# A two-layer fp32 encoder trunk on one core: 48 matmuls of the output projection move between the last units of the latent attention, and the ring of split weight tiles has nine places instead of eight

## The chip, the cores and the metric

One Trainium2 chip, one of its cores. The metric is device time in microseconds of one execution of the whole program, median of several runs.

## The reference

The input is 1024 tokens of width 1024 in fp32. There are two residual layers, each with a mixer and a squared-ReLU MLP of width 4096, and a final norm. The change touches the mixer of the second ("odd") layer: a latent attention of 8 heads beside a recurrent block, whose outputs, 512 wide each, are joined and go through one output projection.

```python
def dense_mla(qn, qr, kn, kr, v):
    ...
        s = (jnp.einsum('bqhd,bkhd->bhqk', qn_b, kn) + jnp.einsum('bqhr,bkr->bhqk', qr_b, kr)).astype(F32) * scale
        p = jax.nn.softmax(s, axis=-1).astype(v.dtype)
        return jnp.einsum('bhqk,bkhd->bqhd', p, v)

def odd_mixer(h, ...):
    ...
    yc = dense_mla(qn, qr, kn, rope(kr), v)
    yd = rglru_block(xr, xg, conv_w, conv_b, wa, ba, wx, bx, lam)
    return jnp.concatenate([yc, yd], axis=-1) @ w_out

def sq_relu_mlp(h, w1, w2):
    u = jax.nn.relu(h @ w1)
    return (u * u) @ w2
...
x = x + mixer(rmsnorm(x, norm_mix))
x = x + sq_relu_mlp(rmsnorm(x, norm_mlp[layer]), w_mlp1[layer], w_mlp2[layer])
```

## The kernel before

Activations lie transposed: 128 channels to a tile, 1024 tokens (S) along it, in two halves of N2 = 512 (`H2`). Results are wanted to fp32, and TensorE is fed in the type fp32r, so every operand is split in two: `split` (L132) writes hi, a cast of x to fp32r (L122, mostly on ScalarE), and lo = x - hi (L130, on VectorE or GpSimd, the latter called POOL in the profile). `mm3` (L179) then makes each product of three matmuls: hi·hi, hi·lo and lo·hi. In the trace a tile whose name ends in h or l is such a half.

The program is five phases: even mixer, MLP 0, odd mixer, MLP 1, final norm. It is written in a framework that tracks tiles: a named pool has a fixed number of places, and a tile that is to be written waits until the place that it gets is free of its former readers. A scheduler orders the instructions within each engine before the program runs, so the order on an engine isn't quite that of the code; on the chip each engine then goes through its own queue strictly in order, and an instruction that waits holds all behind it.

**The ring "w"** has W_BUFS = 8 places of 128 x 1024 fp32r. Through it go: the split weights wh and wl of `fetch` (L168), the weight blocks wb of the MLPs (`block`, L272), and in the attention the head values VS (`head_values`, L1315) and the transposed probabilities cpT (`mla_transpose`). `fetch` also takes one of RAW_BUFS = 2 places for the raw weight, which SP's queue loads by DMA. The list of weights to load (`requests`, from L137) is worked off in order, and `weight` (L164) always has two more ahead of the one it hands out. So o_w_out of m = 0 and m = 1 are split at the beginning of the attention and keep four places through all of it, and in each MLP the last weights of w2 do the same.

**The latent attention** has 32 steps (head h of 8, pair of query blocks p of 4), each of four units kk, so units u = 0 to 127. Each unit issues the pieces of ODD_STEP = ("P", "S", "T", "V"):

- P: a piece of the next head's preparation, up to head 7.
- S: every second unit, the scores of two steps further on (`mla_scores`: six matmuls into the two-bank tile ms, a maximum on VectorE, the exponential e with the sum csm on ScalarE), and in the units between, the normalising of e on POOL (`norm`).
- T: four transposes of e into the PSUM tile ctp, a cast to cpT's first half on ScalarE (L1353) and the difference to its second half on VectorE (L1354).
- V: `av` of the unit four earlier (ODD_LAG = 4): eight matmuls from VS and cpT into the PSUM tile cav (L1124); at the end of every second step a copy cavl on ScalarE (L1131) and a sum into yc.

After the loop stand, in the code, the splits of yd (the recurrent block's output, tiles th to yh and yl, k = 4 to 7; cast on ScalarE, subtraction on POOL), the loads of X (the residual, eight DMAs on SP's queue), `av` of the last four units, the splits of yc (k = 0 to 3), and the projection:

```python
order = [4, 5, 6, 7, 0, 1, 2, 3]
for n in range(2):
    for m0 in range(0, NC, 2):
        W = [self.weight(), self.weight()]
```

For each token half n and each pair of output blocks m it opens two PSUM tiles op, does part 0 (the four k of yd) and part 1 (the four k of yc), 24 matmuls for each m, and adds to X. `done` then squares X for the next norm. The weights are asked for twice over, m = 0 to 7 for n = 0 and again for n = 1.

**The MLPs** are block products with sums and differences of blocks (a scheme of fewer products). Their weights come through `w_stream`, are split to wb (cast on ScalarE L122, difference on VectorE L130) in the ring "w", and are used in twelve matmuls each: in L378 for the first half (PSUM tiles q, copied out to t in L396, among others) and in L498 for the second half (inputs ub).

Of the kernel before, what the change touches and what calls it, by code (L numbers as in the profile page):

```python
# [15 lines left out]
P = 128  # L16
# [30 lines left out]
class Trunk:  # L47
# [89 lines left out]
    def requests(self, ph):  # L137
# [6 lines left out]
        if ph == "odd":  # L144
            idx = {"xr3": 6, "ckv": 2, "cq0": 0, "cq1": 1, "xg0": 7, "xg1": 8, "xg2": 9, "xg3": 10}
            late = {"kn": (a["w_uk"], N2), "qr": (a["w_uq_r"], N2), "qn": (a["w_uq_n"], S), "vn": (a["w_uv"], N2)}
            r = [(a["o_w_in"][i], S, "act" if i != 5 else "pool") for i in (3, 4, 5)]
            seen = set()
            for op in ODD_START:
                k = op[:-1]  # L150
                if k in seen:
                    continue
                seen.add(k)
                if k in idx:
                    r.append((a["o_w_in"][idx[k]], S, "pool"))
                elif k in late:
                    r.append(late[k])
            return r + [(a["o_w_out"][m], S, "act", "pool") for m in range(NC)] * 2
        if ph == "final":
# [8 lines left out]
    def fetch(self, ahead):  # L168

        while self.wreq and len(self.wout) < ahead:  # L170
            src, n, *eng = self.wreq.pop(0)
            raw = self.wp.tile([P, S], F32, tag="raw", name=self.nm("raw"), bufs=RAW_BUFS)
            self.nc.sync.dma_start(raw[:, :n], src)
            h = self.wp.tile([P, S], F32R, tag="w", name=self.nm("wh"))
            l = self.wp.tile([P, S], F32R, tag="w", name=self.nm("wl"))
            self.split(h[:, :n], l[:, :n], raw[:, :n], *eng)
            self.wout.append((h, l))
# [94 lines left out]
    def block(self, tag, x, le="dve", neg=False):  # L272

        nc = self.nc
        w = self.wp.tile([P, S], F32R, tag="w", name=self.nm(tag)) if tag == "wb" else self.G(tag, F32R)
        h, l = w[:, :N2], w[:, N2:]
# [640 lines left out]
    def odd(self, nb, xs, nxt):  # L917
# [195 lines left out]
        def av(u):  # L1113
# [13 lines left out]
            if p % 2 == 1 and kk == 3:  # L1127
                if h % 2 == 0 and p == 1:
# [5 lines left out]
                                        tmp[0:64], op=ALU.add)  # L1134

        prep = iter(())
        for u in range(4 * NS):
            i, kk = divmod(u, 4)
            h, p = steps[i]
            for op in ODD_STEP:  # L1140
# [11 lines left out]
                elif op == "V":  # L1152
                    av(u - ODD_LAG)
                elif op == "P":
                    if p == 0 and kk == 0 and 1 <= h < 7:
                        prep = prep_qk(h + 1)
                    next(prep, None)
            if p == 1 and kk == 3 and h < 7:
                VS[h + 1] = self.head_values(h + 1, Vn)
        Yh, Yl = [None] * 8, [None] * 8  # L1160
        for c in range(4):
            Yh[4 + c], Yl[4 + c] = self.G("yh", F32R), self.G("yl", F32R)
            for s in H2:
                self.split(Yh[4 + c][:, s], Yl[4 + c][:, s], yd[c][:, s], "act", "pool")
        X = self.load_x(xs)
        for u in range(4 * NS - ODD_LAG, 4 * NS):
            av(u)
        for k in range(4):
            Yh[k], Yl[k] = self.G("yh", F32R), self.G("yl", F32R)
# [5 lines left out]
        for n in range(2):  # L1175
            for m0 in range(0, NC, 2):
                W = [self.weight(), self.weight()]
                grp = [(m0 + j, self.PS("op")) for j in range(2)]
                for part in range(2):
                    ks = order[4 * part:4 * part + 4]  # L1180
# [134 lines left out]
    def head_values(self, h, Vn):  # L1315
        nc = self.nc
        VS = self.wp.tile([P, S], F32R, tag="w", name=self.nm("VS"))
        vv = VS.rearrange("p (b t d) -> p b t d", b=8, t=2)
# [25 lines left out]
    def mla_transpose(self, pr, kk):  # L1344
        nc = self.nc
        tp = self.PB("ctp")
        for i in range(2):
            for j in range(2):
                kb = 2 * kk + i
                nc.tensor.transpose(tp[:, (2 * i + j) * P:(2 * i + j + 1) * P], pr[j][:, kb * P:(kb + 1) * P],  # L1350
                                    self.ident)
        pp = self.wp.tile([P, S], F32R, tag="w", name=self.nm("cpT"))
        nc.scalar.copy(pp[:, :N2], tp)  # L1353
# [328 lines left out]
G_BUFS = 41  # L1682
W_BUFS = 8
RAW_BUFS = 2
# [127 lines left out]
```

## Time and profile before

| | |
|---|---|
| median of 3 runs | 2158.83 us (2158.75 to 2159.36) |
| profiled execution, its own time | 2161.66 us |
| its span, first to last instruction | 2159.5 us |
| mean granted TensorE clock | 0.987 |
| TensorE busy | 2051.3 us, 95% of the span |
| VectorE, ScalarE, POOL busy | 71%, 49%, 38% |

The span is what the trace shows; the profiled execution's own time is 2.2 us longer, and 2.8 us longer than the median of the runs without a profile. PE in the profile is TensorE's matmuls and PEld its weight loads, which overlap them; DVE is VectorE, ACT ScalarE, SP the engine whose queue issues the loads. A row of groups gives line, engine, operation, output<-inputs with the count, then shortest, median and longest duration in ns (or busy us and mean ns). In the trace the attention's regular part ends near 1402 us, the projection near 1494 us.

### The profile page before, as it was taken

The page shows a single profiled execution, that of the slowest core. Times are in us where ns is not written, and L with a number is a line of the kernel's source. Part 1 is how long each engine was busy: PE and PEld are TensorE (multiplying, and loading weights), DVE is VectorE, ACT ScalarE, POOL GpSimd, SP SyncE. Part 2 cuts the span into 40 slices and gives each one's busy share as a digit, 9 for nine tenths or more (in the row PEclk, how much of TensorE's full clock was granted, in tenths as well). Part 3 has the DMA queues.
Part 4 walks back from the last instruction along what each step waited for, and adds up shares of the span by engine and source line. Part 5 has one row for each costly group of instructions (what it writes and reads, how often), then busy time and mean ns, then how long its engine had stood idle before and what let it go on. Part 6 is the DMA issues. An engine that isn't in the chain of part 4 may idle for free.

```text
span 2159.5 us, 27248 instructions
## 1 busy us (share of the span) xinstructions
PE 2051.3 (95%) x9600; PEld 1688.1 (78%) x9600; DVE 1542.9 (71%) x2365; ACT 1065.0 (49%) x1853; POOL 823.2 (38%) x635
## 2 busy tenths in 40 slices
PE   6989998999999999999997999999899999999997
PEld 5867776787777888888785898888678777788887
DVE  7688868765656877775898888717875655877964
ACT  5236645444544534340565777734645545544423
POOL 4133332332315142242557776463242321522414
PEclk9999999999999999999999999999999999999999
DMA  5630052543448535132102000245443445654302
GB/s 176 144 136 24 11 185 78 176 166 127 151 152 310 176 107 180 55 101 76 35 25 68 11 11 10 79 130 188 135 172 127 152 155 179 236 204 157 127 29 79
DMA packets 115544, 261.32 MB, mean 121 GB/s; under 512 B 19664, under 2 KB 21840, under 8 KB 115408
## 3 DMA queue, kind: packets, MB, share of 16 engines
q1 hardware_dynamic: 115408, 259.59, 35.7%
q8 instruction: 75, 1.23, 0.2%
q14 instruction: 61, 0.50, 0.1%
HBM read 178.28 MB, written 72.35 MB: 116 GB/s over the span
## 4 chain that ended last, share of the span: by engine, by line
PE 72%; DVE 12%; issue 5%; ACT 5%; DMA 3%; POOL 3%; SPq 0%; POOLq 0%; DVEq 0%; ACTq 0%
PE q L498 22%; PE q L378 22%; PE op L185 7%; PE z L185 6%; PE ms L1334 4%; PE o L185 3%; PE cav L1124 2%; PE ctp L1350 2%; DVE th L1443 1%; POOL acc L245 1%; DVE wb L130 1%; DMA X<-xm 1%; DMA raw<-in_e_w_in_dram 1%; PE tp L870 1%; DVE w L1433 0%
## 5 line engine op out<-in xcount | busy, mean ns | idle before, releaser
L378 PE MATMUL q<-hb,wb 128*128 128x512 f32 x2688 | 629.7, 394 | 34.6 <-DVE wb L130 9.8
L378 PEld LDWEIGHTS q<-hb,wb 128*128 128x128 f32 x2688 | 504.1, 189 | 158.2 <-DVE wb L130 12.8
L498 PE MATMUL q<-ub,wb 128*128 128x512 f32 x2352 | 539.3, 391 | 8.8 <-ACT wb L122 7.0
L498 PEld LDWEIGHTS q<-ub,wb 128*128 128x128 f32 x2352 | 443.2, 189 | 104.3 <-ACT wb L122 8.8
L130 DVE TENSOR_TENSOR wb<-raw,wb 128x512 fp32r<-128x512 f32 x268 | 226.6, 851 | 112.6 <-ACT wb L122 112.2
L122 ACT CAST wb<-raw 128x512 fp32r<-128x512 f32 x268 | 164.3, 619 | 183.0 <-PE q L378 112.7
L122 ACT CAST wb<-sum 128x512 fp32r<-128x512 f32 x152 | 93.8, 620 | 183.3 <-PE q L378 100.7
L130 DVE TENSOR_TENSOR ub<-ut,ub 128x512 fp32r<-128x512 f32 x168 | 136.3, 824 | 66.2 <-ACT ub L122 65.8
L122 ACT CAST ub<-ut 128x512 fp32r<-128x512 f32 x168 | 101.4, 618 | 147.2 <-DVE wb L130 18.8
L130 DVE TENSOR_TENSOR wb<-sum,wb 128x512 fp32r<-128x512 f32 x152 | 126.3, 833 | 22.5 <-ACT wb L122 21.5
L185 PE MATMUL z<-Hh,wh 128*128 128x512 f32 x328 | 129.8, 400 | 10.6 <-ACT wh L122 9.6
L245 POOL TENSOR_TENSOR acc<-acc,sq 128x512 f32<-128x512 f32 (+1 forms) x62 | 88.3, 1427 | 123.3 <-ACT sq L244 121.4
L185 PE MATMUL z<-Hl,wh 128*128 128x512 f32 x328 | 130.2, 397 | 4.1 <-DVE Hl L1471 4.0
L185 PE MATMUL z<-Hh,wl 128*128 128x512 f32 x328 | 129.1, 394 | 0.8 <-DVE wl L130 0.8
L323 POOL TENSOR_TENSOR sum<-raw,raw 128x512 f32<-128x512 f32 x28 | 40.3, 1448 | 215.6 <-DMA raw<-in_w_dram 184.4
L332 POOL TENSOR_TENSOR raw<-raw,raw 128x512 f32<-128x512 f32 x32 | 43.5, 1360 | 203.2 <-DVE wb L130 175.6
L1124 PE MATMUL cav<-cpT,VS 128*128 128x256 f32 x512 | 102.7, 305 | 3.6 <-ACT cpT L1353 2.3
L122 ACT CAST wh<-raw 128x1024 fp32r<-128x1024 f32 (+1 forms) x49 | 49.8, 1015 | 111.9 <-PE z L185 39.4
L1334 PE MATMUL ms<-Kt,Qt 128*128 128x512 f32 (+1 forms) x384 | 99.8, 396 | 2.2 <-ACT e L1341 1.4
L185 PE MATMUL op<-yh,wh 128*128 128x512 f32 x252 | 100.0, 398 | 1.4 <-DVE ya L887 0.9
L185 PE MATMUL op<-yl,wh 128*128 128x512 f32 x252 | 98.9, 393 | 0.0
L185 PE MATMUL op<-yh,wl 128*128 128x512 f32 x252 | 98.0, 393 | 0.0
(343 smaller groups left out, 3815.0 us busy)
## 6 DMA issues: line engine op xcount, KB each, us to landing
raw<-in_w_dram SPq DMA_DIRECT2D x140, 512.0 KB, 4.5
xm<-X SPq DMA_DIRECT2D x32, 256.0 KB, 2.0
X<-xm SPq DMA_DIRECT2D x16, 512.0 KB, 6.6
raw<-in_o_w_out_dram SPq DMA_DIRECT2D x16, 512.0 KB, 3.5
raw<-in_o_w_in_dram SPq DMA_DIRECT2D x11, 512.0 KB, 3.5
raw<-in_e_w_in_dram SPq DMA_DIRECT2D x10, 512.0 KB, 5.1
X<-in_x_dram SPq DMA_DIRECT2D x16, 256.0 KB, 5.6
raw<-in_e_w_out_dram SPq DMA_DIRECT2D x8, 512.0 KB, 3.6
```

Source lines behind the costliest of these rows:

```text
L122: self.nc.scalar.copy(out, x)
L130: e.tensor_tensor(out, x, y, op=ALU.subtract)
L185: self.nc.tensor.matmul(ps, l, r, start=(first and i == 0), stop=(last and i == n - 1))
L245: (eng or nc.gpsimd).tensor_tensor(acc, acc, sq, op=ALU.add)
L323: add(x, blk(p, 1, 0), blk(p, 1, 1), op=ALU.add)
L332: add(x, x, blk(p, 1, 0), op=ALU.add)
L378: nc.tensor.matmul(ps, a, b, start=(first and c == 0 and i == 0), stop=(c == 3 and i == 2), skip_group_check=True)
L498: nc.tensor.matmul(ps[m], a, b, start=(first and j == 0 and i == 0), stop=(j == len(pairs) - 1 and i == 2), skip_group_check=True)
L870: nc.tensor.transpose(tp[:, h * P:(h + 1) * P], pt[h // 2][:, o:o + P], self.ident)
L1124: nc.tensor.matmul(ACC[0][:, (p % 2) * 256:(p % 2 + 1) * 256], VS[h][:, kb * P:(kb + 1) * P], pp[:, t * N2 + ii * 256:t * N2 + (ii + 1) * ...
L1334: nc.tensor.matmul(ps[:, s], l[rows, qs], r[rows, s], start=(i == 0), stop=(i == 2))
L1350: nc.tensor.transpose(tp[:, (2 * i + j) * P:(2 * i + j + 1) * P], pr[j][:, kb * P:(kb + 1) * P], self.ident)
```

## The change

Four things are changed.

1. The splits of yd (k = 4 to 7, in halves) are issued from the loop, in the even units 96 to 110, instead of after it.
2. In the units 105, 109, 113 and 117 `out_weights` loads for m = 0 to 3 the second half of o_w_out[m], which is the four k of yd, as 128 x 512, and splits it into a tile ow (hi in the first half of the tile, lo in the second) of the general pool, which has 41 places, not of the ring. `requests` in turn asks only for the first halves of these four weights (N2 wide) for n = 0, and as before for all else.
3. From unit 120 on, P calls the generator `out_early`, which opens two PSUM tiles of two banks each, and does part 0 of n = 0 for m = 0 to 3: 48 matmuls, six to a call; what is left follows behind the last `av`. The projection takes these four tiles over and does only part 1 in them.
4. W_BUFS is 9.

```diff
+            return r + [(a["o_w_out"][m][:, :N2], N2, "act", "pool") for m in range(4)] + \
+                [(a["o_w_out"][m], S, "act", "pool") for m in [*range(4, NC), *range(NC)]]
...
+        def y_split(c, s):
+            if s.start == 0:
+                Yh[4 + c], Yl[4 + c] = self.G("yh", F32R), self.G("yl", F32R)
+            self.split(Yh[4 + c][:, s], Yl[4 + c][:, s], yd[c][:, s], "act", "pool")
+
+        def out_weights(m):
+            raw = self.H2("owr", "owr")
+            dma(raw, a["o_w_out"][m][:, N2:])
+            w = self.G("ow", F32R)
+            self.split(w[:, :N2], w[:, N2:], raw, "act", "pool")
+            early[m] = [w]
+
+        def out_early():
+            two = [self.PS2("op"), self.PS2("op")]
+            for m in range(4):
+                w = early[m][0]
+                ps = two[m // 2][:, (m % 2) * N2:(m % 2 + 1) * N2]
+                early[m].append(ps)
+                for k in range(4):
+                    cs, lo = slice(k * P, (k + 1) * P), slice(N2 + k * P, N2 + (k + 1) * P)
+                    self.mm3(ps, [(w[:, cs], w[:, lo], Yh[4 + k][:, H2[0]], Yl[4 + k][:, H2[0]])], k == 0, False)
+                    if k % 2:
+                        yield
...
+                    if 96 <= u < 112 and u % 2 == 0:
+                        y_split((u - 96) // 4, H2[u // 2 % 2])
+                    if 104 <= u < 120 and u % 4 == 1:
+                        out_weights((u - 104) // 4)
+                    if u >= 120:
+                        next(fill, None)
...
+                ready = n == 0 and m0 < 4
+                grp = [(m0 + j, early[m0 + j][1] if ready else self.PS("op")) for j in range(2)]
+                for part in range(1 if ready else 0, 2):
...
-W_BUFS = 8
+W_BUFS = 9
```

The scheduler takes these up in its own order. Three places of it follow. A row is line, operation, output<-inputs, size, and a count where rows repeat; numbers behind names count tiles, and lines of the changed kernel from 160 on are one to 34 higher.

ScalarE's queue near the splits of head 7's values (VS), in the attention's last third. Before:

```order
L1321 CAST VS_11843<-Vn_9483 128x2x64
L1321 CAST VS_11843<-Vn_9505 128x2x64
L1353 CAST cpT_11871<-ctp_11866 128x512
L1353 CAST cpT_11885<-ctp_11880 128x512
L1131 COPY cavl_11933<-cav_11781 64x512
L1341 ACTIVATE e_11948,csm_11945<-ms_11936,cnb_11944 128x1024
L1341 ACTIVATE e_11989,csm_11986<-ms_11977,cnb_11985 128x1024
```

And now:

```order
L1355 CAST VS_11855<-Vn_9483 128x2x64
L1355 CAST VS_11855<-Vn_9505 128x2x64
L1375 ACTIVATE e_11880,csm_11877<-ms_11868,cnb_11876 128x1024
L122 CAST ow_11896<-owr_11894 128x512
L1387 CAST cpT_11887<-ctp_11882 128x512
L1387 CAST cpT_11906<-ctp_11901 128x512
L1375 ACTIVATE e_11927,csm_11924<-ms_11915,cnb_11923 128x1024
L1132 COPY cavl_11956<-cav_11791 64x512
L1387 CAST cpT_11934<-ctp_11929 128x512
L122 CAST yh_11959<-th_9062 128x512 x2
L1387 CAST cpT_11948<-ctp_11943 128x512
```

The two exponentials that stood in a row behind the copy cavl now stand apart, with two casts of cpT between them, and the casts of ow and yh stand among those of cpT.

TensorE's queue in the last units of the attention, where no scores are left. Before, with the beginning of the projection at the end of the piece:

```order
L1124 MATMUL cav_12240<-cpT_12237,VS_11843 128x256 x3
L1124 MATMUL cav_12240<-cpT_12250,VS_11843 128x256
L1350 MATMUL ctp_12269<-ident,e_12112 128x128
L1350 MATMUL ctp_12269<-ident,e_12153 128x128
L1350 MATMUL ctp_12269<-ident,e_12112 128x128
L1350 MATMUL ctp_12269<-ident,e_12153 128x128
L1124 MATMUL cav_12240<-cpT_12250,VS_11843 128x256 x3
L1124 MATMUL cav_12240<-cpT_12262,VS_11843 128x256 x4
L185 MATMUL op_12377<-yh_12281,wh_9376 128x512
L185 MATMUL op_12377<-yl_12282,wh_9376 128x512
```

And now, some units earlier:

```order
L186 MATMUL op_12224<-yh_11667,ow_12078 128x512
L186 MATMUL op_12224<-yh_11764,ow_12078 128x512
L186 MATMUL op_12224<-yl_11765,ow_12078 128x512
L186 MATMUL op_12224<-yh_11764,ow_12078 128x512
L186 MATMUL op_12224<-yh_11864,ow_12078 128x512
L1384 MATMUL ctp_12197<-ident,e_11975 128x128
L1384 MATMUL ctp_12197<-ident,e_12022 128x128
L1384 MATMUL ctp_12197<-ident,e_11975 128x128
L1384 MATMUL ctp_12197<-ident,e_12022 128x128
L1125 MATMUL cav_12160<-cpT_12157,VS_11855 128x256 x3
L186 MATMUL op_12224<-yl_11865,ow_12078 128x512
L1125 MATMUL cav_12160<-cpT_12176,VS_11855 128x256
```

Matmuls op on the tiles ow stand between the transposes and the value products, where before only these two followed each other up to the projection. In the whole of the new order all 48 of them, and 26 of the second part of m = 0 and 1, stand ahead of the last value product.

ScalarE's queue where the attention ends and the projection begins; raw is a weight as loaded, wh its first split half, yc the attention's output. Before:

```order
L1353 CAST cpT_12250<-ctp_12245 128x512
L1353 CAST cpT_12262<-ctp_12257 128x512
L1353 CAST cpT_12274<-ctp_12269 128x512
L122 CAST wh_12367<-raw_12365 128x1024
L1131 COPY cavl_12337<-cav_12240 64x512
L122 CAST wh_12373<-raw_12371 128x1024
L122 CAST yh_12358<-yc_11932 128x512
```

And now:

```order
L1387 CAST cpT_12330<-ctp_12325 128x512
L1387 CAST cpT_12348<-ctp_12343 128x512
L1387 CAST cpT_12366<-ctp_12361 128x512
L122 CAST wh_12435<-raw_12433 128x512
L122 CAST wh_12441<-raw_12439 128x512
L1132 COPY cavl_12405<-cav_12314 64x512
L245 ACTIVATE sq_12474<-X_12374 128x512
L122 CAST yh_12426<-yc_11955 128x512
```

The weights of m = 2 and 3 are split in the same place, behind the last cpT, but are half as wide now, and both stand ahead of the copy cavl; a square of X stands ahead of the last cast of yh.

More of the change, by code (lines that the diff above doesn't have):

```diff
@@ L157, in requests @@
                     r.append(late[k])
-            return r + [(a["o_w_out"][m], S, "act", "pool") for m in range(NC)] * 2
+            return r + [(a["o_w_out"][m][:, :N2], N2, "act", "pool") for m in range(4)] + \
+                [(a["o_w_out"][m], S, "act", "pool") for m in [*range(4, NC), *range(NC)]]
         if ph == "final":
@@ L173, in fetch @@
             self.nc.sync.dma_start(raw[:, :n], src)
-            h = self.wp.tile([P, S], F32R, tag="w", name=self.nm("wh"))
-            l = self.wp.tile([P, S], F32R, tag="w", name=self.nm("wl"))
+            h = self.wp.tile([P, S], F32R, tag="w", name=self.nm("wh"), bufs=W_BUFS)
+            l = self.wp.tile([P, S], F32R, tag="w", name=self.nm("wl"), bufs=W_BUFS)
             self.split(h[:, :n], l[:, :n], raw[:, :n], *eng)
@@ L274, in block @@
         nc = self.nc
-        w = self.wp.tile([P, S], F32R, tag="w", name=self.nm(tag)) if tag == "wb" else self.G(tag, F32R)
+        w = self.wp.tile([P, S], F32R, tag="w", name=self.nm(tag), bufs=W_BUFS) if tag == "wb" else self.G(tag, F32R)
         h, l = w[:, :N2], w[:, N2:]
@@ L1134, in av @@
                                         tmp[0:64], op=ALU.add)
+        Yh, Yl = [None] * 8, [None] * 8
+        early = {}
+        def y_split(c, s):
[19 more added lines that the diff above has]
+                        yield
+        fill = out_early()
         prep = iter(())
@@ L1159, in odd @@
                 VS[h + 1] = self.head_values(h + 1, Vn)
[L1160 to L1164, printed above, removed]
         X = self.load_x(xs)
@@ L1167, in odd @@
             av(u)
+        for _ in fill:
+            pass
         for k in range(4):
@@ L1177, in odd @@
                 W = [self.weight(), self.weight()]
-                grp = [(m0 + j, self.PS("op")) for j in range(2)]
-                for part in range(2):
+                ready = n == 0 and m0 < 4
+                grp = [(m0 + j, early[m0 + j][1] if ready else self.PS("op")) for j in range(2)]
+                for part in range(1 if ready else 0, 2):
                     ks = order[4 * part:4 * part + 4]
@@ L1316, in head_values @@
         nc = self.nc
-        VS = self.wp.tile([P, S], F32R, tag="w", name=self.nm("VS"))
+        VS = self.wp.tile([P, S], F32R, tag="w", name=self.nm("VS"), bufs=W_BUFS)
         vv = VS.rearrange("p (b t d) -> p b t d", b=8, t=2)
@@ L1351, in mla_transpose @@
                                     self.ident)
-        pp = self.wp.tile([P, S], F32R, tag="w", name=self.nm("cpT"))
+        pp = self.wp.tile([P, S], F32R, tag="w", name=self.nm("cpT"), bufs=W_BUFS)
         nc.scalar.copy(pp[:, :N2], tp)
```

## The prediction

> **What bounds the kernel now.** I read the first part of the page, then the busy time by stretch of the latent attention, then the chain of waits inside it.
>
> ```profile
> span 2159.5 us, 27248 instructions
> PE 2051.3 (95%) x9600; PEld 1688.1 (78%) x9600; DVE 1542.9 (71%) x2365; ACT 1065.0 (49%) x1853; POOL 823.2 (38%) x635
> ```
>
> TensorE is the bound, and time can be won only where it stands. The chain of waits through the middle of the attention gives its pace there (start, length, what):
>
> ```profile
> 1258.92 1.39 PE ms L1334 x6
> 1260.31 0.12 PE cav L1124
> 1260.43 0.43 PE ctp L1350 x4
> 1260.87 0.48 PE cav L1124 x4
> 1261.34 0.44 PE ctp L1350 x4
> 1261.78 0.36 PE cav L1124 x3
> 1262.14 1.39 PE ms L1334 x6
> ```
>
> From one score group (ms) to the next are 3.22 us: 1.39 us of scores and two units of four transposes (ctp) and four value products (cav), (3.22 - 1.39) / 2 = 0.915 us each. Nothing stands between the pieces. Now the count of matmuls in four stretches, first all engines, then the scores alone:
>
> ```profile
> 1190.00:1310.00 120.00, 119.50 (x800) 108.73 (x799) 105.61 (x200) 92.15 (x176) 89.52 (x97) 1.00 0.07 12
> 1310.00:1380.00 70.00, 68.04 (x451) 60.27 (x450) 57.20 (x107) 51.80 (x100) 33.41 (x39) 1.00 0.05 12
> 1380.00:1402.00 22.00, 18.37 (x121) 15.45 (x120) 16.78 (x28) 18.24 (x35) 12.18 (x10) 0.92 0.44 168
> 1412.00:1440.00 28.00, 28.00 (x125) 23.21 (x124) 3.75 (x6) 7.27 (x10) 16.93 (x9) 1.00 0.51 160
> ```
>
> ```profile
> 1190.00:1310.00 120.00, 61.70 (x240) 1.00 0.07 12
> 1310.00:1380.00 70.00, 31.14 (x120) 1.00 0.05 12
> 1380.00:1402.00 22.00, 0.00 (x0) 0.92 0.44 168
> ```
>
> The columns are length, then busy time of PE, PEld, DVE, ACT and POOL, granted clock, DMA share and GB/s; the second fence has PE's scores only. By the pace above, 1190 to 1310 holds 240/6 x 1.39 + (800-240)/8 x 0.915 = 119.7 us of work in 120: full. 1310 to 1380 holds 20 x 1.39 + (451-120)/8 x 0.915 = 65.7 in 70: **4.3 us lost**. 1380 to 1402, the last units, with no scores left, holds 121/8 x 0.915 = 13.8 in 22: **8.2 us lost**, much of which the busy column hides, because a matmul in a broken row is drawn longer. The projection behind it is full (28.00 of 28.00).
>
> **The part of the early rows: the tail.** The change puts 48 projection matmuls (m 0 to 3, k 4 to 7, first column half), and in the new order also 26 of the second part, between the transposes and value products of these last units. They need neither ScalarE nor VectorE in between. Their pace and the supply:
>
> ```profile
> 1407.79 53.07 PE op L185 x234
> ```
>
> 53.07 / 234 = 0.227 us each, so 74 of them are 16.8 us of work for a hole of 8.2. The other engines have to serve about 15 units in 13.8 + 16.8 = 30.6 us: one cast and one subtraction each,
>
> ```profile
> L1353 ACT CAST cpT<-ctp x128: 572/586/614, 1190.1 to 1402.0; 128x512 fp32r<-128x512 f32 x128
> L1354 DVE TENSOR_TENSOR cpT<-ctp,cpT x128: 664/690/693, 1190.7 to 1402.6; 128x512 fp32r<-128x512 f32 x128
> ```
>
> that is 15 x 0.59 = 8.9 us of ScalarE and 10.4 of VectorE; with eight splits of yc (about 0.6 and 0.7 each) 14 and 16 of 30.6. PE is bound there. I leave 0.7 us of the hole, since its first transpose group still ends in a wait: **gain 7.5**, between 5 and 8.2.
>
> Part of the hole is the clock:
>
> ```profile
> 1391.00:1396.00 5.00, 3.43 (x28) 2.98 (x27) 4.62 (x7) 4.77 (x10) 2.30 (x2) 1.00 1.01 401
> 1396.00:1400.00 4.00, 3.81 (x19) 3.28 (x19) 3.94 (x7) 2.51 (x6) 0.00 (x0) 0.57 0.73 294
> 1395.71 0.99 PE L1124 MATMUL cav<-cpT,VS 128*128 128x256 f32 x4 [1.02 <-DVE cpT L1354]
> ```
>
> After five microseconds in which PE was busy for 3.43, and in which its longest single wait was 1.02 us, the granted clock fell to 0.57 for four; that cost 4.00 x 0.43 = 1.7 us, which the 7.5 contain. I take it that a full PE keeps its clock. The Trainium skill, page "TensorE: Matmul & The Clock Gate", section "What's actually happening", has the clock fall after one idle window of about 3.4 us. The trace disagrees: no wait came near that. By that rule thin filling is not what dropped the clock, so filling would not return it, and the sum would be 1.7 us later, 2150.3.
>
> **The order of the attention.** With nine places, five instead of four are left beside the four tiles of m 0 and 1, which wait through the whole attention. The new order has one score group for every two units almost throughout; the old one has runs without scores, and behind them two exponentials (e) that stand after a copy (cavl) in ScalarE's queue. What that costs, in the chain:
>
> ```profile
> 1366.92 0.03 ACT cavl L1131
> ...
> 1367.53 0.33 ACT e L1341
> ...
> 1368.55 0.20 ACT e L1341
> 1368.79 1.65 PE ms L1334 x6
> ```
>
> PE gets its scores only when the exponential has freed a bank. In the new order this stand is gone, and the 4.3 us with it; what is late next is ScalarE itself. Into units 96 to 123 come the twelve casts of yh and ow, half a row each:
>
> ```profile
> 1384.51 1.14 ACT L122 CAST yh<-th 128x512 fp32r<-128x512 f32 x2
> ```
>
> 12 x 0.57 = 6.8 us in 24 units (12 pairs, 38.6 us), where ScalarE has 23% free (92.15 of 120 above), 8.9 us. It fits closely. The eight POOL subtractions of yl (1.28 us each, in the rows of the join below) and four of ow meet a POOL that is busy 33.41 of 70 there. Each cast of yh delays the cpT cast behind it on ScalarE by up to 1.14 us, and PE's value product waits for that if the transposes ahead don't cover it. I leave 1.2 us: **gain 3.1**, between 0 (all of it comes back as such waits) and 4.3.
>
> **The join.** What the old order had as cover, it now lacks. Of m 0 and 1, 48 matmuls (10.9 us) stood behind the last transposes and hid the loading of the next weights; now their work is done earlier, and m 2 and 3 follow at once, with half their matmuls. Their casts stand behind the last cpT on ScalarE, and the loads of m 4 and 5 wait for the two raw places which m 2 and 3 hold. Prices:
>
> ```profile
> L122 ACT CAST wh<-raw x16: 1045/1054/1057, 1402.4 to 1492.6; 128x1024 fp32r<-128x1024 f32 x16
> L130 POOL TENSOR_TENSOR wl<-raw,wh x14: 2385/2398/4201, 1403.6 to 1478.5; 128x1024 fp32r<-128x1024 f32 x14
> DMA to landing us min/median/max: 3.4/4.1/11.2
> L130 POOL TENSOR_TENSOR yl<-th,yh x8: 1275/1283/1305, 1383.3 to 1392.0; 128x512 fp32r<-128x512 f32 x8
> ```
>
> From the end T of the last transposes: ScalarE's cpT cast to T+0.6, halves of wh for m 2 and 3 to T+1.2 and T+1.7; POOL's halves of wl (as yl, 1.28) to T+2.4 and T+3.7. PE has eleven value products and two matmuls on wh, 11 x 0.12 + 2 x 0.227 = 1.8 us, and waits 0.6 for wl of m 2. Then 22 matmuls to T+7.4. The raw place of m 2 is free at T+2.4: load 3.8 (between 3.4 and 4.1), cast 1.05, subtraction 2.40 give wh of m 4 at T+7.25 and wl at T+9.65; wh of m 5 comes at T+8.9, behind a square. PE does two matmuls on wh of m 4, waits to T+8.9 for wh of m 5 (1.0), and 0.3 more for wl of m 4. After that 22 matmuls (5.0 us) cover the next subtraction. **Loss 2.0**, between 0 (the loads land early) and 5 (a load takes 3 us longer behind the loads of X; the row's longest is 11.2).
>
> **The ring in the two MLPs.** There too w2's last weights hold four places, so the stream has five instead of four. PE's waits for its blocks over the whole span:
>
> ```profile
> PE q L378 <- DVE wb L130: 9.8, 6, 3.4
> PE q L498 <- ACT wb L122: 7.0, 4, 2.6
> PE q L378 <- ACT wb L122: 2.8, 4, 0.9
> PE q L378 <- ACT t L396: 4.2, 4, 2.0
> 673.69 0.62 ACT L122 CAST ub<-ut 128x512 fp32r<-128x512 f32 x1 [5.65 <-DMA ut<-ut_3T]
> ```
>
> The first three are 19.6 us, the most that could come back. But the 2.6 us one is no matter of places: ScalarE stands at 673.69 for a transfer with the wb cast behind it. I take **gain 1.5**. Casts that stand a place earlier can also hold up the copies out of PSUM (fourth row), so the bounds are 4 gained and 3 lost (not quite the 4.2 again). Everything else (the halved splits, four more DMAs on SP's queue ahead of X, the PSUM places that follow) is at nothing: in the projection PE is full and covers it, and uncovered it would be a load's 4 us once.
>
> **Sum.** 7.5 + 3.1 - 2.0 + 1.5 = 10.1 us. The profiled execution took 2161.66 us for its span of 2159.5; 2161.7 - 10.1 = 2151.6. The median shown is 2158.83, 2.8 below the profiled one, so I predict 2151.6 - 2.8 = **2148.8 us**. About 0.2% (4.3 us) is what a measurement of this kernel can tell from no change.
>
> **Rivals.**
> - *The join takes more.* Each late load at T stops PE, since nothing else is left for it. For it: SP's queue has eight loads of X right ahead, and 401 GB/s were moved in the row at 1391. Against: those loads ended within 12 us then, and the tail now lasts 30. Loss 5 for 2.0: 2151.8; with the tail's gain at its low end too, 2154.3. Chance 0.14.
> - *ScalarE becomes the bound in units 96 to 123.* For it: 6.8 us into 8.9 free; POOL and PE wait behind it. Against: a fifth place lets the transposes run ahead. The 3.1 are gone and 2 us of new waits come: 2148.8 + 5.1 = 2153.9. Chance 0.12.
> - *Slower: the ring puts wb casts ahead of the copies t (line 396) in ScalarE's queue,* in both MLPs:
>
> ```profile
> L396 ACT COPY t<-q x32: 567/577/584, 321.1 to 1802.1; 128x512 f32<-128x512 f32 x32
> L122 ACT CAST wb<-raw 128x512 fp32r<-128x512 f32 x268 | 164.3, 619 | 183.0 <-PE q L378 112.7
> ```
>
> A cast that waits for its place (112.7 us of ScalarE's idle time is of that kind) with a copy behind it holds PE's bank. If each of the 32 copies came one cast, 0.62 us, later, that were 19.8 us: 2148.8 + 1.5 + 19.8 = 2170.1 (the gain of 1.5 gone, the loss in its place). It comes out slower by over 0.2% (2163.1) from (2163.1 - 2150.3) / 0.62, about 21 of the 32, on. Against: PE waited for t four times, and one place more makes a cast wait less. Chance 0.05.
> - *It is given back, or is not done.* The first blocks of the second MLP may not be ready ten microseconds sooner, since their loads wait for tiles that the projection frees; PE then stands there for what it saved: 2155 to 2160. Chance 0.07.
>
> **The numbers.** The forecast has 0.62: all terms near their values, 2143 to 2153. The two rivals that leave half lie mostly faster than 2154.5 (0.14 and 0.12, of which 0.06 is not), so faster is 0.62 + 0.20 = 0.82; same 0.06 + 0.06 = 0.12; slower 0.06. With all terms at their good ends (8.2 + 4.3 + 4) it were 2142.4, with tail, order, join and ring at their bad ends (5 + 0 - 5 - 3) 2161.9. These ends don't meet; leaving out 2 in 10, the range is 2143 to 2157.
>
> **What would show it.** Between the last score group and the last value product PE should be busy throughout at a clock of 1.00, with matmuls of the name ow in it. In the last third of the attention a score group should come every 3.2 us, with no wait for e or cpT over half a microsecond. At the join I expect waits of PE for wl and wh of about 2 us in all. PE's waits for wb should add up to 15 to 19. I am wrong if PE stands for cpT behind casts of yh, if the clock falls in the tail in spite of the filling, or if the projection ends ten microseconds earlier and the next MLP does not.

## The result and the profile after

The changed kernel took 2173.09 us, median of 4 runs (2172.0 to 2179.45), against 2159.1 us for the kernel before (4 runs, 2158.75 to 2160.83): a ratio of 1.0068, 95% interval 1.0051 to 1.0085. It is slower by 0.7%; the prediction was 2148.8 us, faster.

The first lines of the page of the changed kernel:

```profile
span 2171.8 us, 27279 instructions
PE 2051.3 (94%) x9600; PEld 1690.2 (78%) x9600; DVE 1555.8 (72%) x2365; ACT 1058.7 (49%) x1857; POOL 824.7 (38%) x639
```

TensorE does the same work in the same busy time, in a span 12.3 us longer. So the question is again where it stands. First the place that the change was about, the busy time by stretch from 1317 us to the last score group, and from there to the last value product (length, then busy time of PE, PEld, DVE, ACT, POOL, granted clock, DMA share, GB/s):

```profile
1317.00:1386.20 69.20, 69.20 (x474) 63.39 (x472) 60.70 (x115) 59.49 (x113) 51.81 (x54) 1.00 0.07 20
1386.20:1416.80 30.60, 30.58 (x188) 26.65 (x186) 17.01 (x28) 15.77 (x29) 4.43 (x4) 1.00 0.40 155
```

Both are full, at a clock of 1.00. The time went elsewhere, and the waits of TensorE over the whole span say where (total, times, longest; L379 is line 378 of before, and t is written in what was L396):

```profile
PE q L379 <- ACT t L397: 35.4, 10, 11.6
PE q L379 <- ACT wb L122: 7.8, 11, 0.9
PE q L379 <- DVE wb L130: 0.3, 1, 0.3
```

The waits for t, the copy that frees a PSUM bank in the first half of each MLP, were 4.2 us in the kernel before and are 35.4 now: one of 11.6 at the start of the second MLP, one of 6.8 at the start of the first (where before stood 3.4 for a block and 2.0 for t), six of 2.6 to 2.7, and two under 1. The waits for a block wb from VectorE, 9.8 us before, are gone: the ninth place did what it is for, and something else came late.

A count over the whole span makes the balance. For each stretch of the trace I take its length less the matmuls in it, each at the pace that it has in a full stretch (0.227 us for 128x512, 0.915 for a unit of four transposes and four value products, 1.39 for a score group; the trace has 512 value products in 128 units, so four to a unit and not eight). What is left is the time lost to TensorE there. It is good to about 1 us, since the last digit of the paces moves a row by that much. The kernels other than the first two are described in the next section.

| us lost in | before | changed | ring nine alone | changed, ring eight | as that, VS moved | as that, PSUM places |
|---|---|---|---|---|---|---|
| first MLP, first half | 30.3 | 39.0 | 40.8 | 30.1 | 30.3 | 28.0 |
| attention, first to last score group | 9.3 | 6.0 | 5.5 | 11.1 | 6.1 | 7.4 |
| its last units | 8.3 | 0.6 | 8.3 | 0.9 | 0.6 | 0.6 |
| projection | 0.3 | 2.6 | 0.2 | 2.3 | 3.0 | 3.4 |
| 40 us behind its last row | 8.8 | 15.8 | 10.8 | 16.7 | 17.9 | 8.8 |
| second MLP, rest of its first half | 16.1 | 21.8 | 24.8 | 14.2 | 16.7 | 19.3 |
| all else | 99.3 | 100.0 | 101.4 | 98.7 | 97.0 | 95.4 |

From before to changed, the attention and its last units gain 11.0 us and the projection gives 2.3 back. The MLPs' first halves lose 14.4 (8.7 and 5.7), and the 40 us behind the projection's last row lose 7.0 more.

**The place in the MLPs.** VectorE's queue of the changed kernel in the first MLP, with the same piece of POOL's queue, and then the chain of waits behind it:

```profile
511.32 0.68 DVE L420 TENSOR_TENSOR u<-q,t 128x512 f32<-128x512 f32 x1
511.92 1.41 DVE L130 TENSOR_TENSOR wb<-raw,wb 128x512 fp32r<-128x512 f32 x1
513.25 1.78 DVE L130 TENSOR_TENSOR wb<-sum,wb 128x512 fp32r<-128x512 f32 x1
514.95 1.77 DVE L130 TENSOR_TENSOR wb<-raw,wb 128x512 fp32r<-128x512 f32 x1
516.65 0.68 DVE L425 TENSOR_TENSOR t<-t,q 128x512 f32<-128x512 f32 x1
```

```profile
511.48 1.30 POOL L343 TENSOR_TENSOR sum<-sum,raw 128x512 f32<-128x512 f32 x1 [8.63 <-DVE wb L130]
512.73 1.75 POOL L328 TENSOR_TENSOR sum<-raw 128x512 f32<-128x512 f32 x1
514.56 1.61 POOL L329 TENSOR_TENSOR sum<-sum,raw 128x512 f32<-128x512 f32 x1
```

```profile
517.36 0.64 ACT t L383
...
518.55 0.58 ACT t L397
519.13 0.04 issue
519.17 3.03 PE q L379 x12
```

Three subtractions of wb stand in a row between the subtractions u and t. They take 1.41 to 1.78 us instead of 0.69, and POOL forms sums of blocks at the same time, from which the next blocks are made. (Of these subtractions of wb in the whole trace, the 282 that no POOL instruction overlaps took at most 0.70 us.) So t comes 5.3 us behind u; ScalarE's activations of t and the copy behind them follow, and TensorE waits 2.8 us at 519.17. Such a wait is counted here from the start of the last matmul ahead of it to the start of the next, less the pace of 0.227; the profile, which draws a matmul 0.39 us long, lists it as 2.66. The same happens at 561.4 and 605.2, and three times in the second MLP.

In the kernel before the same piece of VectorE's queue has one subtraction between the two, and t comes 2.7 us behind u:

```profile
509.81 0.69 DVE L419 TENSOR_TENSOR u<-q,t 128x512 f32<-128x512 f32 x1 [0.80 <-PE q L378]
510.47 1.61 DVE L130 TENSOR_TENSOR wb<-sum,wb 128x512 fp32r<-128x512 f32 x1
512.53 0.69 DVE L424 TENSOR_TENSOR t<-t,q 128x512 f32<-128x512 f32 x1 [0.45 <-PE q L378]
```

There VectorE waits for TensorE and not the other way round. In the order of the program, where numbers count tiles, the piece reads before:

```
L130 TENSOR_TENSOR wb_4399<-raw_4200,wb_4399 128x512
L419 TENSOR_TENSOR u_785_4371<-q_4318,t_780_4320 128x512
L130 TENSOR_TENSOR wb_4418<-sum_4375,wb_4418 128x512
L424 TENSOR_TENSOR t_780_4320<-t_780_4320,q_4319 128x512
L130 TENSOR_TENSOR wb_4438<-raw_4200,wb_4438 128x512
```

and with nine places:

```
L419 TENSOR_TENSOR u_785_4371<-q_4318,t_780_4320 128x512
L130 TENSOR_TENSOR wb_4399<-raw_4200,wb_4399 128x512
L130 TENSOR_TENSOR wb_4418<-sum_4375,wb_4418 128x512
L130 TENSOR_TENSOR wb_4438<-raw_4200,wb_4438 128x512
L424 TENSOR_TENSOR t_780_4320<-t_780_4320,q_4319 128x512
```

Two blocks more stand between u and t: 4438, which has a place sooner, and 4399, which has moved behind u.

**The place behind the projection.** TensorE's queue of the changed kernel at the end of the projection:

```profile
1488.64 8.32 PE L379 MATMUL q<-hb,wb 128*128 128x512 f32 x36
1496.80 0.39 PE L186 MATMUL op<-yh,wh 128*128 128x512 f32 x1
...
1499.29 0.39 PE L186 MATMUL op<-yh,wl 128*128 128x512 f32 x1
1499.52 7.19 PE L379 MATMUL q<-hb,wb 128*128 128x512 f32 x31
1506.55 0.95 PE L221 MATMUL q<-ones,acc 128*128 128x1 f32 x8
1507.36 4.16 PE L379 MATMUL q<-hb,wb 128*128 128x512 f32 x17
1511.35 1.05 PE L232 MATMUL rb<-ident,rr 128*128 128x128 f32 x8
1523.97 1.65 PE L379 MATMUL q<-hb,wb 128*128 128x512 f32 x3 [11.56 <-ACT t L397]
```

The last 12 matmuls of the projection (m 7, second half of the tokens) run 8.2 us late, behind 36 products of the next MLP. The norm of the second half can only begin with them. The products in front were to cover that norm; now 31 + 17 = 48 are left for it, and TensorE stands 11.6 us. In the kernel before, only two products stand ahead of the end of the projection, and 32 + 14 + 24 = 70 behind it:

```profile
1484.33 0.62 PE L378 MATMUL q<-hb,wb 128*128 128x512 f32 x2
...
1492.57 7.42 PE L378 MATMUL q<-hb,wb 128*128 128x512 f32 x32
1499.83 0.95 PE L220 MATMUL ss<-ones,acc 128*128 128x1 f32 x8
1500.64 3.48 PE L378 MATMUL q<-hb,wb 128*128 128x512 f32 x14
1503.95 1.05 PE L231 MATMUL q<-ident,rr 128*128 128x128 f32 x8
1505.43 6.00 PE L378 MATMUL q<-hb,wb 128*128 128x512 f32 x24 [0.42 <-ACT wb L122]
```

VectorE's queue of the changed kernel shows what m 7 waited for:

```profile
1491.88 1.21 DVE L130 TENSOR_TENSOR wl<-raw,wh 128x1024 fp32r<-128x1024 f32 x1
1493.01 0.68 DVE L1220 TENSOR_TENSOR X<-op,X 128x512 f32<-128x512 f32 x1
```

The sum of m 6 into X (L1220) reads op at 1493.01, and m 7's matmuls go into the other half of the same two-bank tile: in the program they carry a wait for VectorE, and have the tile's name. In the kept traces the last twelve rows carry this wait in the changed kernel and in kernels 2 and 12 below, and not in the kernel before, 7 and 11.

```
L186 MATMUL op_12960<-yl_12427,wh_12842 128x512
L186 MATMUL op_12960<-yh_12426,wl_12843 128x512
...
L186 MATMUL op_12960<-yh_12408,wh_12848 128x512 [waits DVE_49]
L186 MATMUL op_12960<-yl_12409,wh_12848 128x512
```

`PS` hands out PSUM in a cycle of eight places, of which the last four are halves of two-bank tiles. Before, the last pair of rows was op_12942 and op_12943, two tiles. The early rows take four steps fewer through `PS`, so every tile behind them has moved by four places.

### The profile page after: what moved, and what is told of

It is laid out like the page before. It is cut to its first block, busy times and chain, and to the rows that moved or that the text cites. A ratio compares the mean times of both kernels' runs of the same rounds, so it can differ in the third digit from the quotient of the medians.

```text
span 2171.8 us, 27279 instructions
## 1 busy us (share of the span) xinstructions
PE 2051.3 (94%) x9600; PEld 1690.2 (78%) x9600; DVE 1555.8 (72%) x2365; ACT 1058.7 (49%) x1857; POOL 824.7 (38%) x639
## 4 chain that ended last, share of the span: by engine, by line
PE 76%; DVE 10%; ACT 5%; issue 3%; POOL 3%; DMA 2%; SPq 0%; POOLq 0%; DVEq 0%; ACTq 0%
PE q L379 23%; PE q L499 21%; PE z L186 7%; PE op L186 7%; PE o L186 4%; PE ms L1368 4%; PE cav L1125 3%; PE ctp L1384 2%; DVE wb L130 2%; POOL acc L246 1%; PE gt L186 1%; DVE X L1562 1%; ACT wb L122 1%; PE tp L871 1%; DMA raw<-in_e_w_in_dram 1%
## 5 line engine op out<-in xcount | busy, mean ns | idle before, releaser
L379 PE MATMUL q<-hb,wb 128*128 128x512 f32 x2688 | 633.3, 396 | 53.9 <-ACT t L397 35.4
L379 PEld LDWEIGHTS q<-hb,wb 128*128 128x128 f32 x2688 | 507.1, 190 | 178.0 <-ACT t L397 42.8
L130 DVE TENSOR_TENSOR wb<-raw,wb 128x512 fp32r<-128x512 f32 x268 | 241.9, 908 | 85.2 <-ACT wb L122 84.4
L130 DVE TENSOR_TENSOR wb<-sum,wb 128x512 fp32r<-128x512 f32 x152 | 138.1, 911 | 56.4 <-ACT wb L122 55.9
L343 POOL TENSOR_TENSOR sum<-sum,raw 128x512 f32<-128x512 f32 x32 | 44.4, 1386 | 198.6 <-DVE wb L130 198.6
L1388 DVE TENSOR_TENSOR cpT<-ctp,cpT 128x512 fp32r<-128x512 f32 x128 | 87.2, 687 | 16.6 <-ACT cpT L1387 14.3
L1387 ACT CAST cpT<-ctp 128x512 fp32r<-128x512 f32 x128 | 74.2, 586 | 39.7 <-PE ctp L1384 39.1
```

The lines of the kernel that those rows point to most:

```text
L130: e.tensor_tensor(out, x, y, op=ALU.subtract)
L343: add(x, x, blk(p, 0, 1), op=ALU.add)
L379: nc.tensor.matmul(ps, a, b, start=(first and c == 0 and i == 0), stop=(c == 3 and i == 2), skip_group_check=True)
L1388: nc.vector.tensor_tensor(pp[:, N2:], tp, pp[:, :N2], op=ALU.subtract)
```

## The experiments

Twelve kernels, each timed in five rounds beside the kernel before. Ratios are against that kernel on the same chip, with 95% intervals.

**1. The ring alone.** The kernel before with one number changed (its edit also names W_BUFS at the tiles of the ring, as the changed kernel does; kernel 2, which names it with eight places, has the MLPs of before):

```diff
-W_BUFS = 8
+W_BUFS = 9
```

> The kernel before with nothing changed but the ring of split weights, nine places for eight (no early rows, the splits of yd where they were). Theory A, the ninth place does the harm in the two MLPs, where VectorE and ScalarE take up blocks wb sooner and the copies t out of PSUM later: the MLPs lose here what they lose in the changed kernel (about 9 us in the first, 13 with the start of the second), the attention gains its order (about 4 us) but not the tail (8 us): 2173 to 2179 us, and six waits of TensorE for t of about 2.8 us, three in each MLP. Theory B, the early rows do it (they move the start of the second MLP, and the stall there of 11.7 us is given back time): only the first MLP's 9 us are lost, less the 4 of the order: 2162 to 2166 us.

Measured: 2178.85 us, 1.0085 (1.0070 to 1.0099). Theory A. The first halves of the MLPs lose 40.8 and 24.8 us as in the table (30.3 and 16.1 before). The attention gains its order here and not its tail, and the waits for t are there without any early row:

```profile
PE q L378 <- ACT t L396: 31.9, 12, 6.9
```

**2. The early rows with eight places.**

```diff
-W_BUFS = 9
+W_BUFS = 8
```

> The changed kernel with the ring back at eight places; early rows, moved splits and halved weights stay. Theory A (the ninth place harms the MLPs): both MLPs run as before, the tail gains its 7.6 us, the next weights cost 2 to 3 us, and the order of the attention keeps its loss of about 4.6 or part of it: 2149 to 2155 us, no wait for t over 2 us. Theory B (the early rows cost the second MLP its start): a stall of 8 to 12 us stays at the start of the second MLP, 2157 to 2162 us.

Measured: 2160.44 us, 1.0001 (0.9992 to 1.0010). The MLPs run as before, as theory A has it, and the tail's 7.4 us are gained; but the stall of theory B is there too:

```profile
PE q L379 <- ACT t L397: 14.0, 3, 11.6
```

Both theories hold, each for its own place. What the early rows gain is lost again behind the last row.

**3. The head values out of the ring.** As 2, and

```diff
-        VS = self.wp.tile([P, S], F32R, tag="w", name=self.nm("VS"), bufs=W_BUFS)
+        VS = self.G("VS", F32R)
```

> The changed kernel with the ring at eight places, and the head values VS of the attention in the general pool of 41 places instead of the ring, so that in the attention alone the ring has about the room of nine. Theory A: the MLPs as before, and the attention as in the changed kernel (tail 7.6 and order 4.6 gained, 2 to 3 lost at the next weights): 2148 to 2151 us. Theory B: the start of the second MLP keeps its stall: 2156 to 2160 us. If the general pool becomes too tight, the loads and splits of yh and ow in the attention's last third come late, and TensorE waits there: 2152 to 2160 us with waits before op on ow.

Measured: 2159.11 us, 0.9991 (0.9982 to 1.0001). The attention has the order of nine places (6.1 us lost instead of 11.1), the MLPs that of eight. The stall behind the last row stays (17.9 in 40 us), and with it 2156 to 2160, as theory B said.

**4. All rows of the projection first.** As 3, and in the projection

```diff
+                        with self.tc.high_priority():
                             self.mm3(ps, ...)
                             if part == 1:
                                 nc.vector.tensor_tensor(X[m][:, H2[n]], ps, X[m][:, H2[n]], op=ALU.add)
```

> The kernel with VS in the general pool and the ring at eight, and the projection's part rows and their sums into X marked for the scheduler as high priority, so that on TensorE all 310 of them stand ahead of the first products of the second MLP; until now the last 12 (m 7, second half) stood behind 31 of those products. Theory C, the early rows are given back there: the filler is used up ahead of the last row, the norm starts as late as before and TensorE then stands with nothing left. Moved back, the last row ends 31 x 0.227 = 7 us sooner, the stall for t at the start of the MLP falls from 14.6 us to about 8, and the time from 2159.1 to 2151 to 2154 us. Theory D, what the stall waits for does not begin with the last row (VectorE's eight scalings of X took 8.3 us there, where they took 5.4 before): the stall stays over 12 us and the time at 2157 to 2160.

Measured: 2163.70 us, 1.0012 (1.0004 to 1.0021). Neither. The last row did end 7.1 us sooner (1480.4 for 1487.5), but the time was not gained: from 1478 to 1545 us TensorE waits 8.9 us for t, and 5.9 and 2.1 for blocks wb and hb. The priority had also put rows ahead of the norm of the first half (its broadcast rb came at 1476.5 instead of 1462.3), so the blocks hb and the casts wb behind them on ScalarE came late. This experiment moved two things and decides nothing about the last row.

**5. One subtraction of seven off VectorE.** As 1, and in `w_stream`

```diff
-            return self.block("wb", x)
+            return self.block("wb", x, "pool" if b == "A12" and not second else "dve")
```

> The kernel before with the ring at nine (no early rows), and the subtraction of one block of seven (A12, in the first half of each MLP) on POOL instead of VectorE, so that in every second product two instead of three subtractions of wb stand between u (line 419) and t (line 424) in VectorE's queue. Theory E, the 2.8 us waits for t come from that run on VectorE: they fall under 1.5 us, and with them the time from 2178.9 to 2163 to 2172 us. Theory F, they come from the casts of wb on ScalarE ahead of the copy t: the waits stay at 2.8 and the time at 2175 to 2181 us.

Measured: 2174.73 us, 1.0066 (1.0054 to 1.0079); 2163 to 2172 were expected. The waits did what theory E says: at 520.4, 561.0 and 601.6 us, where kernel 1 waits 2.83 us, this one waits 1.14. VectorE's queue there:

```profile
514.24 0.68 DVE L419 TENSOR_TENSOR u<-q,t 128x512 f32<-128x512 f32 x1
514.84 1.41 DVE L130 TENSOR_TENSOR wb<-raw,wb 128x512 fp32r<-128x512 f32 x1
516.17 1.78 DVE L130 TENSOR_TENSOR wb<-sum,wb 128x512 fp32r<-128x512 f32 x1
517.87 0.67 DVE L424 TENSOR_TENSOR t<-t,q 128x512 f32<-128x512 f32 x1
```

Two subtractions instead of three, t 3.6 us behind u instead of 5.3, and the waits for t fall from 31.9 us to

```profile
PE q L378 <- ACT t L396: 19.7, 10, 10.9
```

In the same count as the table, 8.3 us come back in the first MLP and 5.8 in the second behind their first 50 and 40 us. The beginning of the first MLP loses 4.7 us more and the 40 us behind the projection's last row 1.6. So the profiled execution is 7.1 us under that of kernel 1, the median only 4.1, and not 7 to 16. The time lies in the range of neither theory; the waits decide, and theory F is out: the casts on ScalarE were the same.

**6. The priority alone,** the edit of 4 on the kernel before.

> A control: the kernel before with nothing but the high priority of the projection's rows. Theory C (the priority is worth what stood ahead of the last rows): only two products stood there, 0.5 us, so no change, 2157 to 2160 us. Rival, the priority by itself is worth the gain: 2150 to 2155 us.

Measured: 2170.05 us, 1.0049 (1.0036 to 1.0062), outside both. The priority harms by itself: the broadcast of the first half's norm came at 1484.1 instead of 1467.8, and 18.8 us are lost in the 40 behind the last row. That confirms the reading of 4 as a confounded test.

**7. The PSUM places moved back.** As 3, and ahead of the projection

```diff
         self.set_wide(False)
+        self.pk = 4
```

> The third kernel again (changed kernel, ring at eight, VS in the general pool) with one thing more: the counter that hands out PSUM places is moved on by four before the projection, as if the four tiles of the early rows had been taken there. Without it the last two rows (m 6 and 7, second half) share one two-bank tile, so m 7 waits for VectorE's sum of m 6 and is queued behind 31 products of the MLP; with it they lie in tiles of their own as before, and only two products stand ahead. Theory G (this shift of places is what gives the early rows' time back): the first 40 us behind the last row lose about 9 us as before and not 18, 2149 to 2153 us. Rival H (VectorE's work on the norm sets the start of the MLP whatever the places are): still 15 to 18 us lost there, 2157 to 2161 us.

Measured: 2151.24 us, 0.9959 (0.9947 to 0.9971). Theory G. TensorE's queue at the end of the projection:

```profile
1472.64 0.62 PE L379 MATMUL q<-hb,wb 128*128 128x512 f32 x2
...
1480.63 0.39 PE L186 MATMUL op<-yh,wl 128*128 128x512 f32 x1
1480.86 7.42 PE L379 MATMUL q<-hb,wb 128*128 128x512 f32 x32
1488.11 0.95 PE L221 MATMUL ss<-ones,acc 128*128 128x1 f32 x8
...
1493.71 5.99 PE L379 MATMUL q<-hb,wb 128*128 128x512 f32 x24 [0.42 <-ACT wb L122]
```

Two products stand ahead of the last row instead of 31, and the 40 us behind it lose 8.8 us as in the kernel before.

**8. The early rows alone,** the edit of 7 on kernel 2 (VS in the ring).

> The changed kernel with the ring at eight places (VS in the ring) and the counter of PSUM places moved on by four: the early rows alone, without what came with them. Theory G: the tail's 7.6 us less 2 to 3 at the next weights are kept, 2152 to 2156 us. Rival H: no change against the second kernel, 2158 to 2162 us.

Measured: 2153.94 us, 0.9969 (0.9957 to 0.9981), as theory G has it. The early rows, with the places put back, are worth 0.3%.

**9. The changed kernel with its PSUM places moved back,** ring at nine.

> The changed kernel as it is, ring at nine, with only the counter of PSUM places moved on by four. Theory G: the start of the second MLP loses what it loses with nine places and no early rows (about 11 us in 40, not 16), so 2164 to 2170 us for 2173. Rival H: 2171 to 2176 us. In both, the waits of 2.8 us for t inside the MLPs stay, since the ring is at nine.

Measured: 2174.05 us (six runs, 2168.4 to 2180.1), 1.0067 (1.0053 to 1.0081). By the median it is rival H's; the profiled execution has a span of 2167.9 us and 12.2 us lost in the 40 behind the last row, where the changed kernel has 2171.8 and 15.8. With nine places the runs spread so far that 4 us can't be told: inconclusive. The 2.8 us waits are all there.

**10. A third place for raw weights.** As 7, and `RAW_BUFS = 3`.

> The fastest kernel so far (ring at eight, VS in the general pool, PSUM places moved on) with three places instead of two for raw weights. Theory I (the waits at the beginning of the projection, 0.44 + 1.35 + 0.73 us there, come from the loads of m 4 and 5 that wait for a raw place): the second and third go, 2149 to 2150.5 us. Rival K: the load or the subtraction on POOL is late by itself, the waits stay, 2150.5 to 2152.5 us.

Measured: 2154.20 us, 0.9974 (0.9962 to 0.9985). At its own place theory I is right in part: of the waits at the beginning of the projection the one of 1.35 us is gone, the third stays (0.57 us in the profile of kernel 7, 0.60 here), and the projection loses 1.7 us instead of 3.4. But the layers ahead, which use the same places, are 3.3 us slower up to the first MLP and 3.4 us in its first half. That this is due to the order of their loads was not tested.

**11. The PSUM counter at six instead of four.** As 7, `self.pk = 6`.

> The fastest kernel so far with the counter of PSUM places moved on by six instead of four: then all rows of the projection stand ahead of the products of the MLP on TensorE, and 36 of these, a norm sum and 24 more behind the last. Theory G (what counts is how many products are left as cover behind the last row, and that its places are free): as with four, 2149 to 2153 us. Rival H (the number is a lucky hit of the scheduler's order): anything outside, 2154 to 2162 us.

Measured: 2152.13 us, 0.9955 (0.9942 to 0.9969). As theory G has it: a different order, with all rows ahead of all products, and the same time.

**12. The shift of PSUM places alone,** the edit of 7 on the kernel before.

> The kernel before with nothing but the counter of PSUM places moved on by four ahead of the projection: no early rows, ring at eight. This is the shift that the early rows bring with them, alone. Theory G: the last row (m 7, second half) waits for VectorE's sum of m 6 and stands behind 31 products of the second MLP; the start of that MLP loses about 17 us in 40 instead of 9, and the time is 2167 to 2170 us against 2160 of the kernel before in this call. Rival H (the stall at the start of the MLP comes from the early rows themselves): no change, 2158 to 2162 us.

Measured: 2161.89 us, 1.0007 (0.9998 to 1.0016); 2167 to 2170 were expected. The stall that theory G names is there, with no early row in the program:

```profile
PE q L378 <- ACT t L396: 11.6, 1, 11.6
```

The 40 us behind the last row lose 16.3 us instead of 8.8, and the projection 3.7 instead of 0.3. What I had not foreseen is the other side: with the places so moved, the scheduler put some rows of the projection into the attention's last units, which lose 3.4 us instead of 8.3, and the rest of the second MLP's first half loses 13.2 instead of 16.1. The mechanism is shown, the total was mis-sized.

## Why the prediction was wrong

**The tail** was right: 7.5 us were forecast, the last units lose 0.6 instead of 8.3, and the clock stays at 1.00 there. Kernel 1, without early rows, keeps the loss of 8.3; kernel 2, without the ninth place, has 0.9. So this gain belongs to the early rows.

**The order of the attention** was right: 3.1 forecast, 3.3 measured. It belongs to the room in the ring: kernels 1 and 3 have it, kernel 2 does not. ScalarE as a new bound (the rival with 0.12) did not appear: nothing is lost between 1317 us and the last score group.

**The join** was right: 2.0 forecast. In the changed kernel, from 1400 to 1500 us,

```profile
PE op L186 <- DVE X L1220: 1.1, 1, 1.1
PE op L186 <- POOL wl L130: 0.3, 1, 0.3
```

and 2.3 us more are lost in the projection than before. The first row names a sum into X; the wait lies at 1421, where the forecast had the weights of m 4 and 5 late, and in experiment 10 it went with a third raw place, so it hung on the raw places.

**The ring in the MLPs is the first step that failed**: "I take gain 1.5", with bounds of 4 gained and 3 lost. It lost 8.7 and 5.7 us. The gain that was forecast is there: the waits for blocks, 19.6 us in the three rows of the prediction, are 0.3 + 4.7 + 7.8 = 12.8 us now, less even than the 15 to 19 that it named as a sign. The prediction did read the right danger, as its slower rival, but gave it 0.05, because TensorE had waited for t only four times and a cast with one more place waits less. It looked at ScalarE's queue and priced one cast of 0.62 us for each of 32 copies, 19.8 us. That its 2170.1 us lies near the measured 2173.1 is luck: the size has another make-up. The list of waits before had two more rows for these matmuls, which the prediction does not show:

```profile
PE q L378 <- DVE t L407: 7.0, 9, 0.8
PE q L378 <- DVE u L410: 6.8, 8, 1.4
```

They say that TensorE already waited 17 times for VectorE's sums and differences there. What happens is on VectorE: in some products three subtractions instead of one stand ahead of t, each stretched to as much as 1.78 us, which gives six waits of 2.8 us where before they were about 0.95, and behind four of them a drop of the clock. The bound of 3 us lost was too narrow: it was taken from the waits for t that were there already (4.2 us), where one place more changes the order of the queue, and the new order comes back three times in each MLP.

**The second is the half sentence that put "the PSUM places that follow" at nothing**, "in the projection PE is full and covers it". PE was full, but with products that were needed as cover later. The last row lies on a chain (row, sum into X, squares, norm, scaling, blocks, copy t), and it is the end of that row that counts, not how busy TensorE is ahead of it. In the changed kernel 7.0 us more are lost in the 40 behind it. Not all of that is the places: kernel 1, with neither early rows nor the shift, loses 2.0 more there than before. With eight places in the ring the shift costs 7.9 us there (kernel 2), and 9.1 are given back between kernels 3 and 7; with nine, kernel 9 could not tell. Kernels 2 and 8, which differ in this counter alone, stand 0.3% apart (1.0001 and 0.9969). The rival "it is given back" forecast the place and nearly the size (2155 to 2160; kernels 2 and 3, without the ninth place, gave 2160.4 and 2159.1), but named another mechanism, late loads of the first blocks, and had 0.07.

With both steps put right, kernels 7 and 11 come to 2151.2 and 2152.1 us, 8.8 and 9.1 us under the kernel before beside them (0.41%, 0.29 to 0.53, and 0.45%, 0.31 to 0.58). The sum of the three terms that were right is 7.5 + 3.1 - 2.0 = 8.6 us. That it fits so well is in part chance: by the table, kernel 7 has 7.7 + 1.9 - 3.1 = 6.5 us from these three places, and some 3 more from the rest of the program, "all else" above all, which was not followed up.

The prediction has one slip in its sums: 1.7 us later than 2148.8 is 2150.5, and not 2150.3. Nothing else hangs on it.

Open is why the scheduler bunches the three subtractions: the order shows that it does, and experiment 5 that the run costs most of what is lost there, but not by what reckoning it came about.

## What to carry to other kernels

A buffer that is shared by several phases is changed in all of them: cost one more place where it is not needed with the same care as where it is, by looking up which instruction of each in-order queue will now stand in front of which. A full TensorE is no proof that an edit is covered; ask which rows begin the next dependent chain, and how much independent work is left behind them. An allocator that counts round hands every later tile another place when an earlier one is taken elsewhere; compare waits and tile names at the end of the phase, not only at the edit.

## What the runs showed of the hardware

A subtraction of 128x512 fp32r on VectorE with two inputs in SBUF took 0.69 us alone and 1.77 to 1.78 us beside a POOL sum of the same size, which took 1.6 to 1.75 us instead of 1.3 in the same stretch. The Trainium skill, page "GPSIMD Engine Reference", section "Specifications", says that POOL's SBUF interfaces are shared with VectorE and that instructions of VectorE with two SBUF inputs contend with it. The rows agree, and the price here is a factor of 2.6 for VectorE.

Two waits of the same length had different consequences for the clock. The one at 519.17 us (2.82 us) left it at 1.00; the one at 561.4 us (2.80 us) was followed by 3.41 us at half. The granted clock in the kept traces changes only at steps of 3.41 us. Four such steps of the changed kernel's trace follow, the first two with the first wait, the last two with the second and what came behind it:

```profile
514.42:517.84 3.42, 2.10 (x10) 1.40 (x8) 3.42 (x4) 0.54 (x2) 1.67 (x2) 1.00 0.71 238
517.84:521.25 3.41, 2.08 (x9) 1.74 (x10) 2.65 (x6) 1.77 (x4) 0.00 (x0) 1.00 0.30 113
558.80:562.21 3.41, 0.83 (x4) 0.70 (x5) 2.65 (x6) 2.25 (x4) 0.00 (x0) 1.00 0.49 154
562.21:565.62 3.41, 3.41 (x10) 2.61 (x8) 1.78 (x3) 0.00 (x0) 0.00 (x0) 0.50 0.87 317
```

The first wait is split between two steps, with TensorE busy for 2.10 and 2.08 us of them; the second falls into one, which leaves 0.83. Over all fourteen kept traces, with each matmul at its pace, all 111 steps at full clock in which TensorE was busy for less than 35% were followed by one at half clock, and none of those above 55% was; between the two, both occur. No run here moves one wait against the steps, so this is a reading of the traces and not a test. The cost is 3.41 x 0.50 = 1.7 us on top of the wait, so a wait of 2.8 us costs 2.8 or 4.5 us here.
